# First head's values taken quad by quad beside its keys and queries, first operands in finer steps, decay steps at other ticks

## The chip, the cores and the metric

One core of one Trainium2 chip runs the kernel. The metric is the device time of one execution in microseconds; with several runs their median counts. TensorE (PE) multiplies matrices, VectorE (DVE) and ScalarE (ACT) work on elements, GpSimd (POOL) does some of that too, and SyncE (SP) issues most transfers.

## The reference

One decoder block over 256 tokens of width 2048, all in float32. RMS norm, then one wide projection `w_in` gives queries, keys and values of four heads, a low-rank decay, and gates; gated linear attention runs in chunks of 64 tokens; its normed output is merged with a gated short convolution; an output projection, a second norm and a SwiGLU network follow. What matters here is the attention's front:

```python
proj = jnp.einsum('bsd,de->bse', h, w_in)
(q, k, v, g_out, gk_low, ...) = jnp.split(proj, SPLIT_IDX, axis=-1)
gk = jnp.einsum('bsr,rk->bsk', gk_low, w_gk_up) + b_gk_up
log_g = jax.nn.log_sigmoid(gk.astype(jnp.float32)) / GATE_LOGIT_NORMALIZER
...
bcum = jnp.cumsum(gc, axis=3)
q_dec = qc * jnp.exp(bcum)
k_dec = kc * jnp.exp(-bcum)
scores = jnp.einsum('nbhik,nbhjk->nbhij', q_dec, k_dec)
scores = jnp.where(causal, scores, 0.0)
o_intra = jnp.einsum('nbhij,nbhjv->nbhiv', scores, vc)
```

The decay `log_g` of all heads is needed before the scores of the first head.

## The kernel before

**Split operands.** Each float32 operand is held as a high part and a low part that PE takes. ACT writes the high part (`hi` from `raw`, L238), DVE the low part (`lo`, L243: raw minus hi). `mm3` (L345 to L349) issues three matmuls per product: low by high, high by low, high by high.

**The weight stream.** Weights come in pieces of 512 KB (128 partitions by 1024 numbers) in the order of `stream_list`. `load_piece` (L268) takes a `raw` buffer of five, issues the load on SP and records ACT's `hi`; DVE's `lo` is recorded one piece later (`finish_low`), from six `hi` and five `lo` buffers. `take` keeps five pieces ahead of use. For keys and queries a piece holds four steps of 128 rows by 256 columns, for values two by 512 columns. The first piece alone is loaded and split in two halves.

**x.** The transposed, gain-scaled x stands as `xh` and `xl` (16 steps of 128 by 256). `start` (L512) loads some steps into a `raw` buffer and splits them, ACT for `xh` and DVE for `xl`. `hooks` say ahead of which piece (and which half of it) a `start` is recorded; `split_gkw` does the same for the decay's low-rank weights. `load_x` reads x once more by token (`xq`) for its square sums, which give the row factor `r1` and, spread by a small product on PE, `rb`.

**Ticks.** Every used piece is one tick. `later` and `at` hang a function on a tick. The order of each engine's instructions is then a list, and an engine takes its list in that order.

**The first head.** `mm_cols(["k0", "q0"], ...)` (L474) takes k0 and q0 piece by piece in turn, eight ticks, with the low-rank decay product `gk_chunks` (L579, eight matmuls each time) behind each k piece. The head's values v0 follow through `mm_tok`, eight ticks. At tick 13 `split_low` and `scale_rows` run, at 14 and 15 `decay_logits` (PE writes `zp`, ACT `za`, DVE `zm`), at 17 the Sigmoid, at 19 `log_decay` (Ln, and DVE's sum), at 20 and 21 `sum_decay` (DVE scans), at 22 `tables_within` (DVE copies, Exp into `ek`), at 23 the Exp into `eq`, at 25 `tables_across` (POOL, then Exp into `exk` and `exq`). `decayed` (L751) multiplies them by the head's scaled keys and queries, from tick 27, and `scores` (L759) is at 29 for the first head, 30 for the second. Meanwhile k1, q1 and v1 go through PE.

**Banks.** Keys, queries and values take turns in six PSUM banks; `aux` gives two more in turn, to `gk_ps`, `rb_ps`, `zp`, `sc_ps` and `o_ps`.

The later heads, the gates, the output projection and the feed-forward network follow in the same stream and aren't touched.

## Time and profile before

| what | value |
|---|---|
| median of 3 runs | 1506.32 us (1505.82 to 1508.32) |
| the profiled execution's own time | 1505.39 us |
| its span in the profile | 1503.7 us |
| granted PE clock, mean | 0.998 |
| PE busy | 1488.9 us (99%) |
| DVE busy | 1277.6 us (85%) |
| ACT busy | 862.9 us (57%) |
| first product after the warm-up starts at | 5.45 us |
| first head's scores start at | 94.87 us |

The span runs from the first to the last instruction; the own time has 1.7 us around it. A row of the timeline gives start, duration, engine, line, operation, output and inputs by name, count, and in brackets the idle time before it with what ended it. PE's rows overlap, since a matmul's end is modelled while the next one already runs: what one matmul costs is read from start to start. A row of the waits gives who waited for whom, the total, the number and the longest.

### The profile page before, as it was taken

What the parts mean: (1) busy time and instruction counts of PE and PEld (TensorE: products, weight loads), DVE (VectorE), ACT (ScalarE), POOL (GpSimd) and SP (SyncE); (2) the same over time, 40 slices, a digit from 0 to 9 for tenths busy, and PEclk for the clock granted to TensorE, in tenths of its full rate; (3) what the DMA queues carried; (4) which work ended last, traced back from release to release, by engine and by line L of the source; (5) the groups of instructions that cost most, each with busy time, mean ns of one, the idle gap of its engine ahead of it and who ended that gap; (6) DMA issues with size and microseconds to landing.
All of it is one profiled execution on the core that took longest, in us unless ns stands there. A gap on an engine that the chain in (4) does not pass through costs nothing.

```text
span 1503.7 us, 19350 instructions
## 1 busy us (share of the span) xinstructions
PE 1488.9 (99%) x7057; PEld 1244.0 (83%) x7057; DVE 1277.6 (85%) x1280; ACT 862.9 (57%) x975; POOL 33.1 (2%) x60
## 2 busy tenths in 40 slices
PE   9999999999999999999999999999999999999997
PEld 8989988888887888888888888888888788888886
DVE  5885869979979879966689999999999999999975
ACT  6864546655655655654566756655565556565553
POOL 0010000000000000000000000000000000000000
PEclk9999999999999999999999999999999999999999
DMA  9755557877877877786676777777877777786782
GB/s 312 239 171 171 178 162 257 283 229 234 283 261 232 296 247 248 252 261 214 211 222 214 238 249 252 252 263 226 268 238 238 256 265 273 243 268 224 241 288 84
DMA packets 99984, 358.58 MB, mean 238 GB/s; under 512 B 11476, under 2 KB 11604, under 8 KB 99760
## 3 DMA queue, kind: packets, MB, share of 16 engines
q1 hardware_dynamic: 96656, 346.88, 70.0%
q0 software_dynamic: 2800, 8.89, 2.2%
q10 hardware_dynamic: 432, 1.57, 0.3%
q8 instruction: 55, 0.90, 0.2%
q14 instruction: 41, 0.34, 0.1%
HBM read 351.03 MB, written 2.10 MB: 235 GB/s over the span
## 4 chain that ended last, share of the span: by engine, by line
PE 95%; DVE 2%; issue 1%; ACT 1%; DMA 0%; SPq 0%; DVEq 0%; ACTq 0%
PE fg L347 8%; PE fg L349 8%; PE fg L348 8%; PE dn L347 5%; PE dn L349 5%; PE dn L348 5%; PE gc L347 3%; PE gc L348 3%; PE gc L349 3%; PE wo L347 2%; PE wo L349 2%; PE v L347 2%; PE gb L347 2%; PE wo L348 2%; PE v L348 2%; PE v L349 2%
## 5 line engine op out<-in xcount | busy, mean ns | idle before, releaser
L243 DVE TENSOR_TENSOR lo<-raw,hi 128x1024 fp32r<-128x1024 f32 (+1 forms) x505 | 611.6, 1219 | 114.3 <-ACT hi L238 32.3
L238 ACT CAST hi<-raw 128x1024 fp32r<-128x1024 f32 (+1 forms) x505 | 523.9, 1048 | 272.5 <-PE gb L349 25.9
L238 ACT CAST hi<-x 128x1024 fp32r<-128x1024 f32 x144 | 151.7, 1053 | 263.5 <-DVE x L265 201.0
L243 DVE TENSOR_TENSOR lo<-x,hi 128x1024 fp32r<-128x1024 f32 x144 | 176.1, 1223 | 37.8 <-ACT hi L238 26.3
L347 PE MATMUL dn<-lo,acth 128*128 128x512 f32 (+1 forms) x368 | 140.7, 382 | 1.7 <-DVE h L1043 0.9
L349 PE MATMUL dn<-hi,acth 128*128 128x512 f32 (+1 forms) x368 | 139.9, 380 | 0.0
L348 PE MATMUL dn<-hi,actl 128*128 128x512 f32 (+1 forms) x368 | 139.8, 380 | 0.0
L265 DVE TENSOR_TENSOR x<-x,raw 128x1024 f32<-128x1024 f32 x96 | 117.0, 1219 | 11.3 <-DMA raw<-in_w_in_dram 6.2
L347 PE MATMUL fg<-lo,hh 128*128 128x512 f32 x288 | 112.4, 390 | 0.0
L349 PE MATMUL fg<-hi,hh 128*128 128x512 f32 x288 | 112.2, 390 | 0.0
L348 PE MATMUL fg<-hi,hl 128*128 128x512 f32 x288 | 112.1, 389 | 0.0
L347 PE MATMUL fg<-lo,sh 128*128 128x512 f32 x256 | 101.0, 395 | 0.0
L348 PE MATMUL fg<-hi,sl 128*128 128x512 f32 x256 | 99.9, 390 | 0.0
L349 PE MATMUL fg<-hi,sh 128*128 128x512 f32 x256 | 99.8, 390 | 0.0
L347 PEld LDWEIGHTS dn<-lo,acth 128*128 128x128 f32 x368 | 69.2, 188 | 15.7 <-DVE h L1043 1.7
L349 PEld LDWEIGHTS dn<-hi,acth 128*128 128x128 f32 x368 | 69.2, 188 | 13.3
L348 PEld LDWEIGHTS dn<-hi,actl 128*128 128x128 f32 x368 | 69.2, 188 | 12.9
L347 PEld LDWEIGHTS fg<-lo,hh 128*128 128x128 f32 x288 | 54.1, 188 | 11.7 <-DVE lo L243 0.5
L349 PEld LDWEIGHTS fg<-hi,hh 128*128 128x128 f32 x288 | 54.1, 188 | 11.3
L348 PEld LDWEIGHTS fg<-hi,hl 128*128 128x128 f32 x288 | 54.1, 188 | 11.1
L259 DVE TENSOR_TENSOR raw<-y,x 128x1024 f32<-128x1024 f32 x48 | 58.5, 1219 | 4.4 <-DMA y<-in_w_gu_dram 2.5
L243 DVE TENSOR_TENSOR lo<-y,hi 128x1024 fp32r<-128x1024 f32 x48 | 58.5, 1218 | 4.3 <-ACT hi L238 2.2
(246 smaller groups left out, 3063.4 us busy)
## 6 DMA issues: line engine op xcount, KB each, us to landing
raw<-in_w_in_dram SPq DMA_DIRECT2D x255, 512.0 KB, 4.6
raw<-in_w_gu_dram SPq DMA_DIRECT2D x176, 512.0 KB, 4.4
raw<-in_w_dn_dram SPq DMA_DIRECT2D x88, 512.0 KB, 4.5
x<-in_w_gu_dram SPq DMA_DIRECT2D x32, 512.0 KB, 4.9
y<-in_w_gu_dram SPq DMA_DIRECT2D x32, 512.0 KB, 3.8
raw<-in_w_out_dram SPq DMA_DIRECT2D x32, 512.0 KB, 3.8
y<-in_w_in_dram SPq DMA_DIRECT2D x16, 512.0 KB, 4.6
x<-in_w_in_dram SPq DMA_DIRECT2D x16, 512.0 KB, 4.8
```

Of the source, the lines that this page charges most:

```text
L238: nc.scalar.copy(hi[:, ks, :], raw[:, ks, :])
L243: nc.vector.tensor_tensor(out=lo[:, ks, :], in0=raw[:, ks, :], in1=hi[:, ks, :].bitcast(F32), op=ALU.subtract)
L259: nc.vector.tensor_tensor(out=raw, in0=y, in1=held["x"], op=ALU.add)
L265: nc.vector.tensor_tensor(out=x, in0=x, in1=other, op=ALU.add)
L347: nc.tensor.matmul(ps, lhsT=sh, rhs=ml, start=first, stop=False, skip_group_check=onto)
L348: nc.tensor.matmul(ps, lhsT=sl, rhs=mh, start=False, stop=False, skip_group_check=onto)
L349: nc.tensor.matmul(ps, lhsT=sh, rhs=mh, start=False, stop=last, skip_group_check=onto)
```

## The change

Four edits, all in the head of the program. What is computed stays the same, and PE has the same matmuls.

- The stream takes k0, q0 and two pieces of v0 in turn (a quad of four steps of the contraction), four times. `mm_cols` gets `beside`: it takes the two value pieces after the queries' and puts the low-rank decay product behind the second of them. v0's two banks are thus in use from the start, beside k0's and q0's four. `done` scales keys and queries two ticks after their last piece.
- The first piece is loaded and split in steps of one, one and two, the second in two halves, and x's first four steps in one, one and two. The gain columns are loaded on ACT's queue instead of SP's. `split_gkw` is recorded ahead of piece 3, and x's next quarters ahead of pieces 4, 7 and 11.
- The decay steps: `split_low` 13 to 17, logits 14 and 15 to 18 and 19, Sigmoid 17 to 20, `log_decay` 19 to 21, `sum_decay` 20 and 21 both to 22, tables 22 to 23, Exp 23 to 24; `tables_across` stays at 25. `decayed` and `scores` keep their ticks.
- v0's high and low parts are written at tick 20 instead of straight after its last piece.

```diff
-    first = [p for pair in zip(out[0], out[1]) for p in pair]
-    return first + [p for g in out[2:] for p in g]
+    first = [p for k, q, v, w in zip(out[0], out[1], out[2][0::2], out[2][1::2]) for p in (k, q, v, w)]
+    return first + [p for g in out[3:] for p in g]
...
-                step = n // 2 if i == 0 else n
+                cuts = {0: (0, 1, 2, n), 1: (0, 2, n)}.get(i, (0, n))
...
-                for a in range(0, n, step):
-                    b = a + step
+                for a, b in zip(cuts, cuts[1:]):
...
-    def mm_cols(keys, ah, al, each=None):
+    def mm_cols(keys, ah, al, beside=None, each=None, done=None):
 
         ps = {key: [bank([P, T], f"{key}_{m}") for m in range(2)] for key in keys}
+        if beside:
+            ps[beside] = [bank([P, 512], f"{beside}_{t}") for t in range(NT)]
         for k0 in range(0, KC, 4):
             for key in keys:
                 col_piece(ps[key], take(key, k0), k0, ah, al)
-                if each and key == keys[0]:
+                if done and k0 == KC - 4:
+                    later(2, lambda key=key: done(key, ps[key]))
+                used()
+            for k in (k0, k0 + 2) if beside else ():
+                piece = take(beside, k)
+                for t in range(NT):
+                    tok_piece(ps[beside][t], t, piece, k, k == 0, k == KC - 2, whole(ah, al))
+                if k > k0:
                     each(k0)
                 used()
...
+        if a == 0:
+            nc.scalar.dma_start(cols, cols_in)
         nc.sync.dma_start(xs[:, 0:b - a, :], xt[:, a * T:b * T].rearrange("p (k t) -> p k t", t=T))
-        if a == 0:
-            nc.sync.dma_start(cols, cols_in)
...
-    hooks[(0, 0)] = lambda: start(xs0, 0, 2)
+    hooks[(0, 0)] = lambda: start(xs0, 0, 1)
+    hooks[(0, 1)] = lambda: start(xs0[:, 1:2, :], 1, 2)
     hooks[(0, 2)] = lambda: start(xs0[:, 2:4, :], 2, 4)
-    hooks[(1, 0)] = split_gkw
+    hooks[(3, 0)] = split_gkw
...
-    at(13, split_low)
+    at(17, split_low)
     for i in range(4):
-        at(14 + i // 2, lambda i=i: decay_logits(2 * i))
-    at(17, lambda: nc.scalar.activation(za, za, AF.Sigmoid))
-    at(19, log_decay)
-    at(20, lambda: sum_decay(0))
-    at(21, lambda: sum_decay(4))
-    at(22, tables_within)
-    at(23, lambda: first_exp.append(nc.scalar.activation(eq, eq, AF.Exp, scale=inv).ins))
+        at(18 + i // 2, lambda i=i: decay_logits(2 * i))
+    at(20, lambda: nc.scalar.activation(za, za, AF.Sigmoid))
+    at(21, log_decay)
+    at(22, lambda: sum_decay(0))
+    at(22, lambda: sum_decay(4))
+    at(23, tables_within)
+    at(24, lambda: first_exp.append(nc.scalar.activation(eq, eq, AF.Exp, scale=inv).ins))
     at(25, tables_across)
...
+        if i:
+            values()
+        else:
+
+            at(20, values)
```

The order on the engines. PE first, at the last of the decay's logits `zp`. Before, they stand among the last matmuls of v0 (`v_0`, `v_1` are its two banks):

```order
L347 MATMUL v_0_516<-lo,xh 128x512
L348 MATMUL v_0_516<-hi,xl 128x512
L349 MATMUL v_0_516<-hi,xh 128x512
L670 MATMUL zp<-gks,gus 128x256 x2
L347 MATMUL v_1_517<-lo,xh 128x512
L670 MATMUL zp<-gks,gus 128x256 x2
L348 MATMUL v_1_517<-hi,xl 128x512
```

In the changed program they stand between the third and the fourth piece of k1 (`k_0`, `k_1` are its banks):

```order
L345 MATMUL k_1_696<-xl,hi 128x256
L346 MATMUL k_1_696<-xh,lo 128x256
L347 MATMUL k_1_696<-xh,hi 128x256
L691 MATMUL zp<-gks,gus 128x256 x4
L345 MATMUL k_0_695<-xl,hi 128x256
L346 MATMUL k_0_695<-xh,lo 128x256
L347 MATMUL k_0_695<-xh,hi 128x256
```

All eight logits' matmuls moved from v0 into k1, in two groups of four (the first group stands one piece of k1 earlier). `scores`, at the end of the decay chain, kept its place: behind 60 matmuls of v1.

ACT next, from the Ln's table load to the last Exp, before:

```order
L691 ACT_TABLE_LOAD
L691 ACTIVATE za_501<-za_501 128x2048
L238 CAST hi_822<-raw_821 128x1024
L238 CAST hi_858<-raw_857 128x1024
L238 CAST hi_892<-raw_891 128x1024
L238 CAST hi_927<-raw_926 128x1024
L706 ACT_TABLE_LOAD
L706 ACTIVATE ek_505<-eq_504 128x2048
L238 CAST hi_958<-raw_957 128x1024
L734 ACTIVATE eq_504<-eq_504 128x2048
L238 CAST hi_996<-raw_995 128x1024
L720 ACTIVATE exk_1013<-exk_1013 128x1024
```

And in the changed program:

```order
L712 ACTIVATE za_682<-za_682 128x2048
L238 CAST hi_891<-raw_890 128x1024
L238 CAST hi_929<-raw_928 128x1024
L238 CAST hi_964<-raw_963 128x1024
L238 CAST hi_1003<-raw_1002 128x1024
L238 CAST hi_1030<-raw_1029 128x1024
L727 ACT_TABLE_LOAD
L727 ACTIVATE ek_686<-eq_685 128x2048
L238 CAST hi_1048<-raw_1047 128x1024
L755 ACTIVATE eq_685<-eq_685 128x2048
L741 ACTIVATE exk_1020<-exk_1020 128x1024
L742 ACTIVATE exq_1021<-exq_1021 128x1024
```

The cast between the Exp into `eq` and that into `exk` is gone; the casts between Ln and the first Exp became five. Ahead of the Ln's table load, where two casts stood behind the Sigmoid, one stands now.

DVE last, from the table copies to the first head's products with `eq` and `exq`, before:

```order
L705 COPY eq_504<-bc_503 128x8x64
L243 TENSOR_TENSOR lo_930<-raw_891,hi_892 128x1024
L243 TENSOR_TENSOR lo_961<-raw_926,hi_927 128x1024
L806 TENSOR_TENSOR kr_987<-k1_0_726,rb_114 128x256
L806 TENSOR_TENSOR kr_987<-k1_1_727,rb_114 128x256
L755 TENSOR_TENSOR ek_505<-ek_505,kr_514 128x512
L807 SCALAR_TENSOR_TENSOR qr_988<-q1_0_855,rb_114 128x256
L807 SCALAR_TENSOR_TENSOR qr_988<-q1_1_856,rb_114 128x256
L243 TENSOR_TENSOR lo_999<-raw_957,hi_958 128x1024
L755 TENSOR_TENSOR eq_504<-eq_504,qr_515 128x512
L243 TENSOR_TENSOR lo_1026<-raw_995,hi_996 128x1024
L755 TENSOR_TENSOR exk_1013<-exk_1013,kr_514 128x256
```

And in the changed program:

```order
L726 COPY eq_685<-bc_684 128x8x64
L673 SCALAR_TENSOR_TENSOR qr_997<-q1_0_856,rb_114 128x256
L673 SCALAR_TENSOR_TENSOR qr_997<-q1_1_857,rb_114 128x256
L243 TENSOR_TENSOR lo_1006<-raw_963,hi_964 128x1024
L243 TENSOR_TENSOR lo_1033<-raw_1002,hi_1003 128x1024
L243 TENSOR_TENSOR lo_1051<-raw_1029,hi_1030 128x1024
L776 TENSOR_TENSOR ek_686<-ek_686,kr_632 128x512
L776 TENSOR_TENSOR eq_685<-eq_685,qr_653 128x512
L243 TENSOR_TENSOR lo_1073<-raw_1047,hi_1048 128x1024
L776 TENSOR_TENSOR exk_1020<-exk_1020,kr_632 128x256
L776 TENSOR_TENSOR exq_1021<-exq_1021,qr_653 128x256
L776 TENSOR_TENSOR eq_685<-eq_685,qr_997 128x512
```

The scaling of k1 (`kr_987` before) went ahead of the table copies. Three low parts of weights stand between the last table copy and the product with `eq` in both, now in one run; one stands between the product with `eq` and that with `exk`, as before. Of v1's pieces, `lo_1006` is the fifth's low part.

## The prediction
> **What bounds the kernel now.** I read the page first, then the waits of TensorE (PE), then PE by stage, then the timeline of the start and of the decay steps.

> The page's busy row and the first row of its chain:

> ```profile
> PE 1488.9 (99%) x7057; PEld 1244.0 (83%) x7057; DVE 1277.6 (85%) x1280; ACT 862.9 (57%) x975; POOL 33.1 (2%) x60
> ...
> PE 95%; DVE 2%; issue 1%; ACT 1%; DMA 0%; SPq 0%; DVEq 0%; ACTq 0%
> ```

> PE is busy 99% of 1503.7 us and is 95% of the chain that ended last. The change leaves PE the same matmuls, so only PE's waiting can change. A busy PE isn't a PE at full pace, though, so stretches by the granted clock and count come next:

> ```profile
> 5.45:11.89 6.44, 5.48 (x35) 4.65 (x35) 3.86 (x7) 3.86 (x8) 0.00 (x0) 1.00 0.96 350
> 11.89:58.38 46.49, 46.49 (x300) 42.46 (x301) 33.74 (x52) 35.32 (x58) 0.31 (x1) 1.00 0.93 319
> 58.38:81.41 23.03, 23.03 (x193) 23.03 (x193) 19.17 (x22) 14.54 (x14) 4.29 (x3) 1.00 0.51 147
> 81.41:95.03 13.62, 13.62 (x62) 11.26 (x62) 13.05 (x19) 11.95 (x11) 2.50 (x3) 1.00 0.47 155
> ```

> The columns are PE, weight loads, DVE, ACT, POOL, then clock, DMA share and GB/s. Only the first stretch has idle PE. From 11.89 to 95.03 PE never stops; DVE works 13.05 of the last 13.62 us. So in the start there is something to win, and up to the scores at 95 there is nothing to win and much to lose. The waits of PE say the same: the one in the start is small, and the longest anywhere after the warm-up is 0.9 us.

> ```profile
> PE g L347 <- DVE lo L243: 0.9, 1, 0.9
> ...
> PE k L347 <- DVE xl L519: 0.6, 1, 0.6
> ```

> **The start.** The timeline of the first 13 us, PE and what it waits for:

> ```profile
> 1.26 0.42 SPq L515 DMA_DIRECT2D cols<-in_cols_dram  x1
> 1.27 4.02 PE L500 MATMUL warm_ps<-warm 128*128 128x512 bf16 x9 [1.27 <-DVE spare L496]
> 3.94 0.91 ACT L518 ACTIVATE xh<-xs,cols 128x256 fp32r<-128x256 f32 x2 [1.64 <-DMA cols<-in_cols_dram]
> 5.45 0.80 PE L347 MATMUL k<-xl,hi 128*128 128x256 f32 x2 [0.16 <-ACT hi L238]
> 8.38 0.50 PE L347 MATMUL k<-xl,hi 128*128 128x256 f32 x2 [0.60 <-DVE xl L519]
> 9.10 0.38 PE L348 MATMUL k<-xh,lo 128*128 128x256 f32 x1 [0.23 <-DVE lo L243]
> 11.89 0.38 PE L348 MATMUL q<-xh,lo 128*128 128x256 f32 x1
> 12.23 0.28 PE L348 MATMUL q<-xh,lo 128*128 128x256 f32 x1
> 12.35 0.28 PE L349 MATMUL q<-xh,hi 128*128 128x256 f32 x1
> ```

> From 12.23 to 12.35 a 256-column matmul takes 0.12 us. By 11.89 PE has started 24 of k0, 8 of the decay's low-rank product (gk) and 2 of q0: 34, worth 4.1 us, in 6.44 us. Some 2.3 us are lost, and the warm-up (to 1.27 + 4.02 = 5.29) forbids a start much before 5.45. So **2.4 us is the most the start can give**.

> The new steps let the first quarter of k0 begin as the warm-up ends instead of 0.16 later, but the wait at 8.38 to 9.10 is for the second half of x and of the piece, and ahead of it stand as many bytes as before (two steps of 128 KB in place of each 256 KB). What smaller steps cost in transfer, the trace shows only by its neighbours:

> ```profile
> 3.00:4.00 1.00, 1.00 (x4) 0.40 (x3) 0.00 (x0) 0.06 (x1) 0.46 (x3) 1.00 0.85 265
> ...
> 6.00:7.00 1.00, 1.00 (x7) 0.83 (x6) 0.12 (x1) 0.10 (x1) 0.00 (x0) 1.00 0.87 200
> ```

> At 3 to 4 us rows of 2 KB move at 265 GB/s; at 6 to 7, with the 128 KB of gkw among them, 200. For the 512 KB now cut to 1-KB rows this is 2.6 instead of 1.9 us at worst; nothing at best. I take 0.3, nearer the middle since gkw was only part of the mix. Then the lower half of k0 starts at 9.10 + 0.3 = 9.4, its last ten matmuls take 1.2 to 10.6, and q0 follows at once, because gk now stands behind the values and q0 comes in halves. By 11.89 PE has done 24 + 1.29/0.12 = 35 against 34: **0.1 us won**. The bounds are 0.7 lost (the worst transfer rate, plus a little) and 2.4 won.

> Edits of the start that I cost at nothing: the columns' load on ACT's queue saves SP one 0.42 us issue and delays ACT by about as much, under ACT's 1.64 idle; without that cover, 0.4. The gkw split goes three pieces later and is needed only after the first values. From there each quad gives PE 48 matmuls at 0.12, 24 at 0.23 (13.62 us for the 60 of v1 up to 95.03) and 8 at 0.12, 12.2 us for 2.5 MB, where it had 6.7 us for 1.5 MB: less demand per us than the 350 GB/s above, so no transfer is late.

> **The decay chain.** Here is the larger term. PE's anchors first:

> ```profile
> 51.59 0.64 PE L670 MATMUL zp<-gks,gus 96*128 96x256 f32 x4
> ...
> 56.82 0.40 PE L670 MATMUL zp<-gks,gus 96*128 96x256 f32 x2
> ...
> 58.22 0.28 PE L347 MATMUL k<-xl,hi 128*128 128x256 f32 x1
> ...
> 81.24 0.40 PE L347 MATMUL v<-lo,xh 128*128 128x512 f32 x1
> ...
> 94.87 1.05 PE L766 MATMUL sc_ps<-eq,ek 128*128 128x128 f32 x8
> 95.76 0.61 PE L768 MATMUL sc_ps<-exq,exk 128*128 128x128 f32 x4
> ```

> Now zp, the decay's logits, stands in the middle of v0; the last pair starts at 56.82 and the first head's scores at 94.87: **38.0 us** for everything between. In the new order the last zp stand after three of k1's four pieces. Moving 8 of them behind v0 lets k1 start 1.0 earlier, at 57.2, less the 0.1: 57.1. Two pieces of k1 (48 x 0.12 = 5.8), four zp (0.5), one piece (2.9): the second group begins at 66.3, its last pair at 66.5. That pair waits for the readers of the first group, which use the same two banks. The reader's row in the next fence, 53.94, ends 3.2 after the group's start at 51.59, and one DVE pass over a logit ends some 0.4 later; PE is back after 28 x 0.12 = 3.4. I take 0.1, between 0 and 0.5: last pair at 66.6, **9.7 later** than before. The scores, with the same PE work ahead of them, would come at 94.87 - 0.1 + 0.1 = 94.9. So only 28.3 us remain.

> What the chain needs is in the rows of ACT, DVE and POOL, each of which takes its instructions in the order of its list:

> ```profile
> 53.94 0.87 ACT L673 ACTIVATE za<-zp,cols 128x256 f32<-128x256 f32 x2 [0.32 <-DVE zm L674]
> ...
> 60.57 1.28 ACT L729 ACT_TABLE_LOAD   x1
> ...
> 63.69 1.98 ACT L238 CAST hi<-raw 128x1024 fp32r<-128x1024 f32 x2
> 65.68 1.28 ACT L691 ACT_TABLE_LOAD   x1
> ...
> 83.07 1.28 ACT L706 ACT_TABLE_LOAD   x1 [6.34 <-DVE eq L705]
> ...
> 87.13 1.92 ACT L734 ACTIVATE eq<-eq 128x2048 f32<-128x2048 f32 x1
> 88.94 1.03 ACT L238 CAST hi<-raw 128x1024 fp32r<-128x1024 f32 x1
> 89.88 1.06 ACT L720 ACTIVATE exk<-exk 128x1024 f32<-128x1024 f32 x1
> ```

> ```profile
> 68.92 2.29 DVE L692 TENSOR_TENSOR zm<-zm,za 128x2048 f32<-128x2048 f32 x1 [0.72 <-ACT za L691]
> ...
> 82.16 0.83 DVE L705 COPY eq<-bc 128x512 f32<-128x512 f32 x1
> ...
> 87.98 1.21 DVE L243 TENSOR_TENSOR lo<-raw,hi 128x1024 fp32r<-128x1024 f32 x1
> 89.11 0.68 DVE L755 TENSOR_TENSOR eq<-eq,qr 128x512 f32<-128x512 f32 x1
> ...
> 91.92 0.43 DVE L755 TENSOR_TENSOR exq<-exq,qr 128x256 f32<-128x256 f32 x1 [0.34 <-ACT exq L721]
> ```

> ```profile
> 82.68 1.23 POOL L718 TENSOR_TENSOR exq<-bc 128x512 f32<-128x512 f32 x1
> ```

> From the last zp pair (56.82) to the end of eq x qr (89.11 + 0.68 = 89.79) the chain took 33.0, and to the end of exq x qr (91.92 + 0.43) 35.5. It fitted with 5 us to spare. It isn't loose: each link starts as the one before ends (68.92 on Ln, 83.07 on the copy at 82.16 + 0.83). Fewer ticks between steps therefore don't shorten it; only fewer strangers in the queues do. The new lists take out two: one of the two casts at 63.69 (0.95) and the cast at 88.94 (0.94). The other weight splits stay, one between zm and the scans, one behind the scans.

> So: the Ln sum 68.92 + 9.7 - 0.95 = 77.7; the Exp table load 83.07 + 8.75 = 91.8; **eq x qr 97.9 to 98.5**, where PE is at 94.9. Behind it DVE now has one weight split (1.13, by 87.98 to 89.11), exk (0.4) and exq (0.43): **exq ready at 100.5**. PE's second set of score matmuls would start at 95.76 + 0.0 = 95.8. **4.7 us lost.** Before that the same queue is late once more: the fifth piece of v1 needs a split that stands behind the table copies (91.8 - 0.1) and two scalings of q1, done near 93.6, where PE is at 92.1. So PE would wait 1.5, 2.2 and 1.0 us in three places, one sum of 4.7.

> Bounds of this term: 3.9 if the handovers between engines shrink by 0.8 in all, 5.5 if DVE falls behind by most of one more split (1.13). Nothing takes it back later: PE has no slack behind the scores. POOL's five table operations end at 83.9 now, at 92.7 then, 5 us before exk's Exp at 97.7: hidden. v0's accumulators hold six banks with k0's and q0's; k1 needs k0's, scaled about 7 us ahead of it; v1 needs v0's, read around 70 against 81: hidden, each with over 5 us.

> [...] The 0.9 us wait above left the clock at 1.00. [...]

> **Sum.** 1505.39 (the profiled execution; its span is 1503.7, 1.7 lies around it) - 0.1 + 0.1 + 4.7 = 1510.1. The median shown, 1506.32, is 0.9 above that execution, so I forecast **1511.0** for a median.

> **Rivals.**
> - The chain fits after all (not slower). For: the steps stand closer in ticks, and DVE's 19.17 of 23.03 and ACT's 14.54 leave gaps. Against: the links are chained by data, and the gaps lie in waits for the chain itself. It decides at the slack: last zp pair to exq must shrink from 35.5 to 29.2, and two casts give only 1.9. Then only the start counts: 1506.2, or 1503.9 if the start wins all. Chance 0.14.
> - The change's start wins its full 2.4 with the chain as I say: 1511.0 - 2.3 = 1508.7. It is inside the range and in the forecast's chance.
> - The three waits run together and the clock falls. The start shows the cold pace: 0.80 for two matmuls at 5.45, 0.50 at 8.38. A cold stretch like the start's (1.27 to about 6.2) at half pace costs 2.5: 1513.5. Chance 0.06, as three waits are likelier than one.

> That the instructions stand otherwise than described is no rival: the lists are the program's own.

> **How the numbers follow.** Forecast 0.80. The range runs from 1511.0 - 2.7 (chain 3.9, two of the start's 2.4) to 1511.0 + 2.6 (chain 5.5, start 0.7 lost, or the clock): 1508.3 to 1513.6; it leaves out the first rival and tails. A measurement of this kernel can tell about 0.2%, 3.0 us. Faster than that would need more than the start holds: 0.02. Within: 0.12 of the first rival and 0.03 of the forecast's lower edge, 0.15. Slower: 0.83.

> **What would show it.** After the change: zp in k1; the Exp table load near 92; DVE's eq x qr ending near 98.5; PE waits of about 1.5 on a weight split in v1 and of 2.2 and 1.0 on DVE eq and exq at the scores; k1 starting near 57. I am wrong if PE reaches the scores without a wait, if k1 starts more than 1 us off 57.1, or if the granted clock falls below 1.00 there.

## The result and the profile after

| | before | after |
|---|---|---|
| median of 5 runs each | 1506.32 us (1505.23 to 1508.32) | 1514.21 us (1511.18 to 1515.28) |
| ratio of the times, 95% interval | | 1.0049 (1.0037 to 1.006) |
| the profiled execution's own time | 1505.39 us | 1514.47 us |
| its span | 1503.7 us | 1512.8 us |

The change makes the kernel slower, by 7.9 us of the medians (0.5%; the interval of the ratio lies wholly above 1) and 9.1 us of the two profiled executions. The page of after, its busy row and the first row of its chain:

```profile
PE 1490.8 (99%) x7057; PEld 1243.8 (82%) x7057; DVE 1278.4 (85%) x1282; ACT 863.0 (57%) x977; POOL 33.0 (2%) x60
...
PE 85%; DVE 6%; issue 3%; DMA 2%; ACT 2%; SPq 0%; DVEq 0%; ACTq 0%
```

The busy row tells nearly nothing, as before. In the chain PE's share fell from 95% to 85%, but this row scatters too: the later profiles of the unchanged kernels have 93% and 90% for before and 93%, 93% and 89% for after. The waits of PE in after name the places. Three are new between 90 and 101 us: 1.4 of the first row (its other 0.88 us lies in the start), and the other two rows:

```profile
PE v L345 <- DVE lo L243: 2.2, 2, 1.4
...
PE sc_ps L787 <- DVE eq L776: 1.7, 1, 1.7
...
PE sc_ps L789 <- DVE exq L776: 0.6, 1, 0.6
```

The timeline of after at the points that the prediction named, PE, ACT and DVE:

```profile
57.45 0.28 PE L345 MATMUL k<-xl,hi 128*128 128x256 f32 x1
...
66.57 0.80 PE L691 MATMUL zp<-gks,gus 96*128 96x256 f32 x4
...
92.06 1.28 ACT L727 ACT_TABLE_LOAD   x1 [6.45 <-DVE eq L726]
...
98.05 0.69 DVE L776 TENSOR_TENSOR eq<-eq,qr 128x512 f32<-128x512 f32 x1 [1.20 <-ACT eq L755]
...
92.29 0.39 PE L347 MATMUL v<-hi,xh 128*128 128x512 f32 x1
94.04 0.50 PE L345 MATMUL v<-lo,xh 128*128 128x512 f32 x1 [1.36 <-DVE lo L243]
...
96.67 0.39 PE L347 MATMUL v<-hi,xh 128*128 128x512 f32 x1
98.80 1.16 PE L787 MATMUL sc_ps<-eq,ek 128*128 128x128 f32 x8 [1.74 <-DVE eq L776]
100.61 0.60 PE L789 MATMUL sc_ps<-exq,exk 128*128 128x128 f32 x3 [0.65 <-DVE exq L776]
```

What a wait costs is read from start to start: 92.29 to 94.04 is 1.75, less the 0.23 that a matmul of 512 columns takes, 1.52 us. The bracket says 1.36, since it counts from the modelled end at 92.29 + 0.39. In the same way the three waits are 1.5, 1.9 and 0.8, together **4.2 us**. The first product behind each wait takes another 0.1 us more than usual (94.04 to 94.38, against 0.23).

The same markers in both timelines show where the rest came:

| start of | before | after | later by |
|---|---|---|---|
| k1 (before: less the 1.0 of the zp that stood ahead) | 57.22 | 57.45 | 0.23 |
| v1 | 81.24 | 81.61 | 0.37 |
| the first scores | 94.87 | 98.80 | 3.93 |
| the first head's `o_ps` | 103.02 | 107.97 | 4.95 |
| the first `g` | 204.25 | 209.20 | 4.95 |
| the same `dn` group near the end | 1447.59 | 1456.17 | 8.58 |
| end of the span | 1503.7 | 1512.8 | 9.1 |

Here `o_ps` is the first product of scores and values, `g` a product of the gates and `dn` one of the feed-forward network's last projection. Up to the first `o_ps` the program lost what the start (0.4 up to v1) and the waits explain. Then nothing for 100 us; then 3.6 us between `g` and `dn`, where the lists of all engines are the same in both kernels. The first theory was that the chain is late for its place on PE (C), which explains the 4.95. For the other 4 us there were two rivals: it belongs to the change (P), or it is scatter of single transfers (S). A third one, the clock (H), came only with the second profile of the changed kernel.

### The profile page after: what moved, and what is told of

The parts are those of the page before. It is cut to its first block, busy times and chain, and to the rows that moved or that the text cites. A ratio compares the mean times of both kernels' runs of the same rounds, so it can differ in the third digit from the quotient of the medians.

```text
span 1512.8 us, 19359 instructions
## 1 busy us (share of the span) xinstructions
PE 1490.8 (99%) x7057; PEld 1243.8 (82%) x7057; DVE 1278.4 (85%) x1282; ACT 863.0 (57%) x977; POOL 33.0 (2%) x60
## 4 chain that ended last, share of the span: by engine, by line
PE 85%; DVE 6%; issue 3%; DMA 2%; ACT 2%; SPq 0%; DVEq 0%; ACTq 0%
PE fg L347 7%; PE fg L345 7%; PE fg L346 7%; PE dn L345 4%; PE dn L347 4%; PE dn L346 4%; DVE lo L243 3%; PE gc L345 3%; PE gc L346 3%; PE gc L347 3%; PE wo L345 2%; PE gb L345 2%; PE gb L347 2%; PE gb L346 2%; PE wo L346 2%
## 5 line engine op out<-in xcount | busy, mean ns | idle before, releaser
L243 DVE TENSOR_TENSOR lo<-raw,hi 128x1024 fp32r<-128x1024 f32 (+1 forms) x507 | 612.1, 1214 | 118.1 <-ACT hi L238 34.3
L238 ACT CAST hi<-raw 128x1024 fp32r<-128x1024 f32 (+1 forms) x507 | 524.2, 1045 | 280.1 <-PE gb L347 27.5
L238 ACT CAST hi<-x 128x1024 fp32r<-128x1024 f32 x144 | 151.6, 1053 | 270.9 <-DVE x L265 215.9
L243 DVE TENSOR_TENSOR lo<-x,hi 128x1024 fp32r<-128x1024 f32 x144 | 176.1, 1223 | 36.3 <-ACT hi L238 25.9
L347 PE MATMUL dn<-hi,acth 128*128 128x512 f32 (+1 forms) x368 | 139.9, 380 | 0.0
L347 PE MATMUL fg<-hi,hh 128*128 128x512 f32 x288 | 112.2, 390 | 0.0
L347 PE MATMUL fg<-hi,sh 128*128 128x512 f32 x256 | 99.8, 390 | 0.0
L347 PEld LDWEIGHTS dn<-hi,acth 128*128 128x128 f32 x368 | 69.2, 188 | 13.3
L347 PEld LDWEIGHTS fg<-hi,hh 128*128 128x128 f32 x288 | 54.1, 188 | 11.2
L243 DVE TENSOR_TENSOR lo<-y,hi 128x1024 fp32r<-128x1024 f32 x48 | 58.5, 1219 | 4.6 <-ACT hi L238 2.1
```

Of the source, the lines that this page charges most:

```text
L238: nc.scalar.copy(hi[:, ks, :], raw[:, ks, :])
L243: nc.vector.tensor_tensor(out=lo[:, ks, :], in0=raw[:, ks, :], in1=hi[:, ks, :].bitcast(F32), op=ALU.subtract)
L347: nc.tensor.matmul(ps, lhsT=sh, rhs=mh, start=False, stop=last, skip_group_check=onto)
```

## The experiments

Sixteen runs in five comparisons, each with its own runs of the kernel before on the same chip. "Above before" means the difference of the medians within one comparison.

### Does the later loss belong to the change?

The two kernels, run again without any edit.

> The kernel before, unchanged, a second profile and more times. In the first profile of it PE goes from the start of the first o_ps matmul (103.02) to the start of the last dn group (1447.59) in 1344.6 us; in the changed kernel, whose lists of instructions are the same there, in 1348.2. Theory S (scatter: single transfers that land up to 1 us late at places that differ from run to run): this profile lies anywhere from 1343 to 1349 for the same stretch, with waits of PE over 0.3 us at other places than the first time, and the time 1505 to 1508.5. Theory P (the 3.6 us belong to the change): the stretch takes 1344.6 within 0.6 again, with its waits at the same places.

Measured: 1506.88 us on both sides (ratio 0.9998, 0.999 to 1.0007). The stretch from `o_ps` to `dn` took 1346.4 us, 1.8 longer than in the first profile. The places of the waits were mostly the old ones, against what S said, but their sizes weren't: the one ahead of the last `trb` group but one (transposes on PE) went from 0.5 to 1.5 us.

The second repeat was made later, beside runs on the first steps; theory G, that finer first steps cost about 1 us somewhere behind, is taken up there.

> The kernel before, unchanged, for comparison. All theories: within 0.5 of the other runs of it; theory G: 1243.3 to 1244.7 us from the first g matmul to the last dn group.

Measured: 1507.14, beside 1507.3 for the other runs. One row of the stage view, from the first `g` to the `dn` group, for three kernels: before, this second repeat of before, and after. The columns are length, PE, weight loads, DVE, ACT, POOL, clock, DMA share, GB/s.

```profile
204.25:1447.59 1243.34, 1239.84 (x5527) 1021.43 (x5525) 1098.62 (x1036) 715.12 (x770) 22.20 (x39) 1.00 0.75 248
```

```profile
204.00:1451.10 1247.10, 1241.29 (x5527) 1021.86 (x5525) 1097.74 (x1035) 714.30 (x769) 22.13 (x39) 1.00 0.76 247
```

```profile
209.20:1456.17 1246.97, 1241.36 (x5526) 1021.07 (x5525) 1098.78 (x1035) 713.82 (x768) 22.15 (x39) 1.00 0.76 247
```

The unchanged kernel before can take 1247.1 us for the stretch too: **S holds**, the 3.6 us are within the kernel's own scatter. From the first `o_ps` to `dn` the three profiles of before take 1344.6, 1346.4 and 1348.3 us, and the four of the changed kernel 1348.2, 1347.6, 1345.1 and 1347.4. One piece of the scatter, in before and in after, as DVE waits for a transfer or doesn't (SPq is the issue, DVE the first reader):

```profile
1052.32 0.33 SPq L232 DMA_DIRECT2D y<-in_w_gu_dram  x1
...
1057.04 1.23 DVE L259 TENSOR_TENSOR raw<-y,x 128x1024 f32<-128x1024 f32 x1
```

```profile
1058.42 0.33 SPq L232 DMA_DIRECT2D y<-in_w_gu_dram  x1
...
1064.10 1.23 DVE L259 TENSOR_TENSOR raw<-y,x 128x1024 f32<-128x1024 f32 x1 [0.93 <-DMA y<-in_w_gu_dram]
```

The issue comes 6.1 later in after, as all of PE does there, but DVE's step comes 7.1 later: the transfer landed some 1 us late. DVE is busy 88% of the whole stretch (1098.8 of 1247.0), so it has little room to make that up. Some 60 us on, at 1126.82, PE waits 0.6 for DVE in after and not in before; that this is the same delay come through is argued, not shown.

> The changed kernel, unchanged, a second profile and more times. All theories: the three waits before and at the scores come again at 1.5, 1.9 and 0.8 us within 0.2, and the first o_ps matmul starts 4.9 to 5.0 us later than in the kernel before. Theory S: the stretch from the first o_ps to the last dn group takes anywhere from 1343 to 1349 us, and the median of all its times comes nearer to 4.9 above that of the kernel before (1511.5 to 1512.5). Theory P: the stretch takes 1348.2 within 0.6 again, waits at the same places, and the median stays at 1514.

Measured: 1514.8 us, 7.9 above before, from 1510.5 to 1518.3, and 1347.6 us for the stretch. Taken alone this run is as P wanted it, in the stretch and in the median; it is the repeats of before and the later ones of this kernel that rule P out. The profile had something that no theory expected. Its timeline of PE at the scores:

```profile
57.41 0.28 PE L345 MATMUL k<-xl,hi 128*128 128x256 f32 x1
...
97.45 1.16 PE L787 MATMUL sc_ps<-eq,ek 128*128 128x128 f32 x8 [2.10 <-DVE eq L776]
99.26 1.22 PE L789 MATMUL sc_ps<-exq,exk 128*128 128x128 f32 x4 [0.65 <-DVE exq L776]
...
109.53 0.39 PE L345 MATMUL o_ps<-vl,sch 128*128 128x512 f32 x1
```

and its stages, cut where the clock changes:

```profile
95.21:98.63 3.42, 1.31 (x9) 0.97 (x8) 3.42 (x4) 2.48 (x3) 1.64 (x2) 1.00 0.77 256
98.63:102.04 3.41, 2.78 (x9) 2.39 (x10) 3.41 (x7) 2.14 (x3) 0.00 (x0) 0.50 0.46 165
102.04:105.45 3.41, 3.41 (x10) 2.64 (x9) 2.78 (x5) 0.78 (x2) 0.31 (x1) 0.50 0.67 168
```

The clock is the third number from the end. The wait on the fifth v1 piece is gone and the other two are 2.3 and 0.8 from start to start (3.1 us in all, less than in the first profile), yet `o_ps` comes at 109.53, 1.6 later. The clock column says why: it is 0.50 from 98.63 to 105.45. That is theory H, which all later runs test: **behind the waits the clock falls, in some runs.**

> The changed kernel, unchanged, beside the next two on one chip. Theory H (waits of 3.1 to 4.2 us, and in most runs, not in all, a fallen clock behind them at about 3 us): a median 6.5 to 8.5 above the kernel before, times that spread over more than 3 us, and lower clocks where the time is longer. Theory N (no clock, late transfers): the spread is that of the kernel before.

Measured: 1512.38, 5.0 above before (1509.8 to 1515.7): below the 6.5 to 8.5 of H, but with the wide spread that H wanted (5.9 us, beside 2.4 in the kernel before). In this profile the same rows read:

```profile
57.10 0.28 PE L345 MATMUL k<-xl,hi 128*128 128x256 f32 x1
...
97.15 1.16 PE L787 MATMUL sc_ps<-eq,ek 128*128 128x128 f32 x8 [2.10 <-DVE eq L776]
...
106.33 0.39 PE L345 MATMUL o_ps<-vl,sch 128*128 128x512 f32 x1
```

```profile
92.96:96.37 3.41, 2.09 (x10) 1.39 (x8) 3.41 (x3) 2.67 (x2) 3.41 (x3) 1.00 0.66 217
96.37:99.79 3.42, 2.00 (x14) 1.76 (x15) 3.42 (x6) 3.21 (x4) 0.17 (x1) 1.00 0.69 181
```

Two executions of one kernel, with the same waits (2.1 on eq, 0.65 on exq by the brackets). With the clock at 1.00, k1 to `o_ps` takes 106.33 - 57.10 = 49.2 us; with the fallen clock 109.53 - 57.41 = 52.1. The difference, **2.9 us, is the clock alone**.

> The changed kernel, unchanged, beside the run before. Theory S and H: one of the two patterns of VectorE and GpSimd, waits of 3.1 or 4.2 us with it, and in about two runs of three a clock of 0.997 or less; runs at 0.996 or less 2.5 to 3.5 us above those at 0.998.

Measured: 1511.62, 5.4 above before (ratio 1.0035, 1.0021 to 1.0049). The waits are those of the two repeats before; the clock fell again, this time for 3.4 us, and k1 to `o_ps` takes 50.9, 1.6 more than with a full clock:

```profile
95.81:99.22 3.41, 1.66 (x13) 1.48 (x13) 3.41 (x6) 2.88 (x4) 0.50 (x1) 1.00 0.82 184
99.22:102.64 3.42, 3.42 (x10) 2.75 (x10) 3.42 (x7) 1.56 (x4) 0.00 (x0) 0.50 0.36 137
```

Over all 22 runs of the changed kernel, 15 have a mean clock of 0.997 or less, against 6 of 119 of the kernel before. The 7 at 0.998 are on average 5.1 us above before, the 9 at 0.997 5.9, the 6 at 0.996 or less 8.6: the 3.5 between the first and the last group is at the upper end of what the expectation gave, the middle group is only 0.8 above the first. The mean clock is a coarse gauge here: in the profiles the program's end, behind the last product, lies at half clock for 4.2 to 7.0 us, which alone moves the third digit.

### Take the waits away, or lengthen them

The first edit puts scores and the products with the values one tick later, the second two ticks:

```diff
-        at(max(now + 3, 29 + i), lambda i=i: scores(i))
+        at(max(now + 3, 30 + i), lambda i=i: scores(i))
...
-        tick_of = max(count["tick"] + 1, 31)
+        tick_of = max(count["tick"] + 1, 32)
```

> The changed kernel with the scores and the products with the values one tick (one weight piece, 2.9 us of PE) later, and nothing else. Theory C (the decay chain is late for its fixed place on PE, 4.2 of the 4.9 us): the waits on eq and exq (1.9 and 0.8) go, the wait on the fifth v1 piece (1.5) stays, since its split stands where it stood; the head's end comes 2.7 us earlier than in the changed kernel, and the time is 2.5 to 3 us below it, 2 above the kernel before. Rival D (what PE lacks is DVE's work, so a wait taken away at the scores comes back at the next thing that DVE owes PE): waits of about 2.7 us show again at scr, scl, or a weight split within the next 15 us, and the time is the changed kernel's.

Measured: 1509.39, 2.5 above before (ratio 1.0016, 1.0007 to 1.0025) and 5.4 below the changed kernel in the same comparison, about twice what C expected. The wait on eq is gone, waits of 0.5 on exq and 0.9 on `scr` (the scores as they are copied out of PSUM) were left, and the wait on the fifth v1 piece, which C kept, isn't there, as in the three repeats of the changed kernel. The clock was 0.998 or more in all 11 runs. D in its full form falls: what is left is 1.3 us and the time isn't the changed kernel's. That the gain is more than the waits taken away fits H.

> The changed kernel with the scores and the products with the values two ticks later. One tick later left waits of 0.46 at exq and 0.87 at scr ahead of the values' products, the clock at 0.998, and 1509.4. Theory C+H: no wait over 0.3 us from 90 to 125, and the time is 1506.5 to 1508.2, the kernel before within what a measurement can tell. Rival D (the 2.5 us that were left are not waits at the scores): 1509 to 1510 again.

Measured: 1507.82, 1.5 above before (1.0009, 1.0001 to 1.0018), one wait of 0.7 left, where C+H wanted none over 0.3, and the clock at 0.998 in all 11 runs. The time is as C+H said.

The third edit goes the other way, for the first head's scores alone:

```diff
-        at(max(now + 3, 29 + i), lambda i=i: scores(i))
+        at(max(now + 3, 29 + i) - (i == 0), lambda i=i: scores(i))
```

> The changed kernel with the first head's scores one tick earlier: the products with eq stand 12 matmuls (2.7 us of PE) earlier, those with exq 8. The wait on eq grows to 4.6 to 5.0 us in one piece, that on exq shrinks to under 0.3: 1.9 us more of waiting in all. Theory H: one gap of that length drops the clock in every run, for as long as in the second profile of the changed kernel (6 us at half pace, 3 us lost), so the median is 1.9 us plus the share of runs that keep the clock now, 2.5 to 3.5 above the changed kernel's. Theory N: 1.9 above it, at a clock of 1.00 behind the gap.

Measured: 1516.3, 8.9 above before and 3.9 above the changed kernel in the same comparison, a little over H's range. All 5 runs had a clock of 0.995 or 0.996. The wait and the stages of this profile:

```profile
98.72 2.08 PE L787 MATMUL sc_ps<-eq,ek 128*128 128x128 f32 x8 [6.11 <-DVE eq L776]
```

```profile
93.57:96.98 3.41, 0.00 (x0) 0.00 (x0) 3.22 (x4) 3.41 (x3) 0.00 (x0) 1.00 0.56 150
96.98:100.39 3.41, 1.67 (x8) 1.67 (x9) 2.41 (x4) 3.41 (x4) 0.00 (x0) 0.50 0.82 302
100.39:103.81 3.42, 3.42 (x12) 2.94 (x12) 1.70 (x5) 1.33 (x2) 0.00 (x0) 0.50 0.55 168
```

One gap of 6.1 us: the clock falls 4.4 us into it, at 96.98, and stays down until 103.81, 5.1 us after PE has work again. The wait was 6.1 and not 5.0 since this profile has the long pattern of the decay steps (below).

### Keep the waits, but not the idleness

Throwaway products fill the two waits; PE waits as long for eq and exq as before.

```diff
+        for n in range(16 if i == 0 else 0):
+            nc.tensor.matmul(ps[:, 0:2, :], lhsT=xh[:, n, 0:P], rhs=xh[:, n, :], start=True, stop=True)
         for t in range(NT):
...
+        for n in range(5 if i == 0 else 0):
+            nc.tensor.matmul(ps[:, 2, :], lhsT=xh[:, n, 0:P], rhs=xh[:, n, 0:P], start=True, stop=True)
         for j, m in enumerate(ms):
```

> The changed kernel with throwaway matmuls ahead of the first head's scores, into the scores' own accumulators, which the real ones then overwrite: 16 of 256 columns ahead of eq (about 1.9 us at full pace) and 5 of 128 columns ahead of exq (0.5 us). PE waits as long for eq and exq as before, but isn't idle meanwhile. Theory H (a part of the loss is the clock: in the second profile of the changed kernel, after waits of 2.1 and 0.65 us, the granted clock is 0.50 to 0.66 from 98 to 106, which costs about 3 us): the clock stays at 1.00 there in the profile and the time falls by 2 to 3 us below the changed kernel's, to 1511.5 to 1512.8. Theory N (the clock falls for another reason, or the rest is late transfers): the time stays at 1514 to 1515.

Measured: 1511.48, 5.1 above before. The stages of the scores in its profile:

```profile
93.23:96.65 3.42, 3.42 (x23) 3.11 (x22) 3.42 (x3) 2.51 (x2) 3.42 (x3) 1.00 0.82 200
96.65:100.06 3.41, 3.07 (x23) 2.67 (x22) 3.41 (x6) 3.37 (x4) 0.01 (x1) 1.00 0.58 156
```

PE is never idle for long and the clock stays at 1.00. From k1 to the first `o_ps` the profile takes 49.2 us, as long as the second repeat of the changed kernel, which had the same waits and kept its clock: what the throwaway products can save is the clock and nothing else. The time is where H put it, but the changed kernel wasn't run on that chip, so it was run again beside it.

> The changed kernel with throwaway matmuls in the waits ahead of the first head's scores, again, now with the changed kernel beside it on the same chip. Theory H: the clock is 0.998 or 0.999 in nearly all its runs and its median 1.5 to 3 below the changed kernel's. Theory N: its median is that of the changed kernel within 0.8.

Measured: 1511.82, 4.4 above before, only 0.6 below the changed kernel of that comparison: that is N's outcome, and not the 1.5 to 3 of H. The changed kernel had 0.998 in 4 of its 6 runs there, so there was less to win; by the medians of this comparison alone H isn't shown. What stands is the clock: 13 of the 15 runs with filled waits have 0.998 or more, against 7 of 22 without.

### What decides whether the clock falls

The stages quoted here are cut at the changes of the clock, and they have one length: behind the waits the clock was low for 3.41 or 6.83 us, never for another time. Counted in steps of 3.413 us from the moment at which the clock first rose in that execution (5.67 in after, 6.47 in its first repeat, 4.21 in the second), every fall and rise lies on a step (from the first rise to the fall at the end of the program after takes 1501.86 us, 440 steps, and before 1491.62, 437). So cut, the two cells of after that hold its waits read:

```profile
94.42:97.83 3.41, 2.64 (x12) 1.84 (x10) 2.43 (x3) 3.41 (x3) 0.00 (x0) 1.00 0.70 209
97.83:101.25 3.42, 1.80 (x13) 1.61 (x14) 3.20 (x6) 3.42 (x5) 0.00 (x0) 1.00 0.82 268
```

The cell with the least work of PE near the scores (from 80 to 130 us) in each profile, and the clock in the cell behind it:

| profile | PE busy in its emptiest cell of 3.41 us | clock in the next |
|---|---|---|
| scores one tick earlier | 0.00 | 0.50 |
| GpSimd held back (below) | 1.19 | 0.50 |
| after, first repeat | 1.31 | 0.50 |
| decay's ticks alone (below) | 1.32 | 0.50 |
| after, third repeat | 1.66 | 0.50 |
| after | 1.80 | 1.00 |
| coarse start (below) | 1.90 | 1.00 |
| after, second repeat | 2.00 | 1.00 |
| filled waits, second time | 2.19 | 1.00 |
| scores one tick later | 2.70 | 1.00 |
| filled waits, first time | 3.07 | 1.00 |

So it is in all eleven profiles with waits at this place: where PE was busy for 1.66 us or less in a cell at full clock, the next had 0.50, and where it was busy for 1.80 or more, 1.00. Behind the waits the clock rose again after a cell that was nearly full: not after 1.67 (scores one tick earlier) or 2.78 (after, first repeat), but after 3.05 (GpSimd held back), 3.23 (decay's ticks alone), 3.41 and 3.42. At the start of the programs it rose after 3.26 in before and 3.41 in after, elsewhere once after 2.94 (after, second repeat) and once after 2.99, but not after 3.08 and 3.21 in two others, so busy time alone doesn't tell the rise. Since the cells began at another moment in each execution, the same waits fell into one cell (1.31 in the first repeat of after) or were shared by two (2.09 and 2.00 in the second). The limit for the fall, between 1.66 and 1.80, was read from these rows, and no run was made to test it, but the rest of the traces does. All 18 profiles together have 7886 such cells at full clock. The 23 with half clock behind them (5 at these waits, 18 at the ends of the programs) hold 0.00 to 1.66 us of work, and every other one holds 1.80 or more (in before 437 cells, the last with 0.04 and the others with 2.48 or more; in after 440, the last with 0.00 and the others with 1.80 or more).

### One part of the change alone

The decay's ticks alone, in the kernel before, with the old order of pieces and the old start:

```diff
-    at(13, split_low)
+    at(17, split_low)
     for i in range(4):
-        at(14 + i // 2, lambda i=i: decay_logits(2 * i))
-    at(17, lambda: nc.scalar.activation(za, za, AF.Sigmoid))
-    at(19, log_decay)
-    at(20, lambda: sum_decay(0))
-    at(21, lambda: sum_decay(4))
-    at(22, tables_within)
+        at(18 + i // 2, lambda i=i: decay_logits(2 * i))
+    at(20, lambda: nc.scalar.activation(za, za, AF.Sigmoid))
+    at(21, log_decay)
+    at(22, lambda: sum_decay(0))
+    at(22, lambda: sum_decay(4))
+    at(23, tables_within)
...
```

> The kernel before with only the decay's steps moved to the ticks of the changed kernel; the values behind keys and queries and the first steps as before. Theory C+H (the whole loss is the late chain, as waits of 3 to 4.3 us in all and as a fallen clock behind them): about the changed kernel's time, 1512.5 to 1515, with waits on eq and exq at the scores. Rival Q (the values side by side, or the finer steps, cost a share of their own): 1509 to 1511.5, waits or not.

Measured: 1511.55, 5.2 above before (1.0031, 1.0019 to 1.0042): below C+H's range in absolute terms, at Q's upper edge, but as far above before as the changed kernel was in its last two comparisons. All 6 runs had a clock of 0.997. From k1 to the first `o_ps` its profile takes 51.1 us, 5.3 more than before (there less the 1.0 of `zp`): the whole loss. PE waits 0.3 on eq and 0.5 on exq by the brackets, and longest on a weight split of v1, where C+H had the waits at the scores. The longest wait and the stages behind it:

```profile
94.25 0.50 PE L347 MATMUL v<-lo,xh 128*128 128x512 f32 x1 [2.09 <-DVE lo L243]
```

```profile
92.07:95.48 3.41, 1.32 (x6) 1.05 (x6) 3.41 (x5) 3.19 (x3) 1.04 (x1) 1.00 0.20 23
95.48:98.90 3.42, 3.23 (x8) 1.97 (x6) 3.36 (x4) 3.42 (x4) 0.00 (x0) 0.50 0.72 280
```

A single wait of 2.1 us was enough here, and the clock fell 1.2 us after PE had work again.

The other four runs are about the first steps. First the changed kernel with the first steps of before (cuts in halves for k0 only, q0 whole, two chunks of x, the columns on SP):

```diff
-                cuts = {0: (0, 1, 2, n), 1: (0, 2, n)}.get(i, (0, n))
+                cuts = (0, n // 2, n) if i == 0 else (0, n)
...
-    hooks[(0, 0)] = lambda: start(xs0, 0, 1)
-    hooks[(0, 1)] = lambda: start(xs0[:, 1:2, :], 1, 2)
+    hooks[(0, 0)] = lambda: start(xs0, 0, 2)
```

> The changed kernel with the first steps of before: k0's first piece in two halves, q0's whole, x two chunks at a time, the columns on SP's queue; the quads and the decay's new ticks stay. Theory C+H: the start is worth under 1 us either way, the waits at the scores and the fallen clock are as in the changed kernel, and the time is 1513.5 to 1515.5. Rival Q (the finer steps cost a share): 1511.5 to 1513.

Measured: 1512.05, 5.7 above before (1.0032, 1.0021 to 1.0044), the two waits at 2.1 and 0.65, the clock below 0.998 in 3 of 6 runs. k1 starts at 58.15, 0.7 to 1.3 later than in the four profiles of the changed kernel (56.85 to 57.45): with the values side by side, the finer steps do win that much (in the last run below, coarse too, k1 starts at 58.01). They win it against the coarse quads, though, not against the old order, where k1 starts at 56.8 to 57.2, less the `zp`. The time lies in Q's range and not in that of C+H, but it is about as far above before as the changed kernel in two of its comparisons (5.0 and 5.4), and the changed kernel wasn't run on this chip: no share of the finer steps can be read from it.

Then the finer steps alone in the kernel before (`cuts`, the two `start` hooks and the columns on ACT's queue as in the change, nothing else), in two comparisons:

> The kernel before with the finer first steps alone: k0's first piece in three parts and q0's in two, x in steps of one chunk at first, the columns on ACT's queue; the order of the pieces, the values behind keys and queries, and the decay steps as before. Theory C: no wait at the scores; the second group of k0 matmuls starts 0.3 to 0.8 us earlier than 14.62, and the time is 1505.5 to 1506.3, no difference that a measurement of the time can tell. Rival F (the finer steps themselves cost transfer rate): the second group of k0 starts later than 14.62, by up to 0.7, and the time is up to 1507.

> The kernel before with the finer first steps alone, once more: its 1.0 above the kernel before (from 0.5 below to 2.1 above) was not told from no change. Theory G (the finer steps cost about 1 us, not at the start but in later waits): 0.7 to 1.5 above the kernel before again, and 1244.7 to 1246 us from the first g matmul to the last dn group. Theory S (scatter): within 0.6 of the kernel before.

Measured: 1.0 above before (1.0006, 0.9997 to 1.0014) and 0.8 below (0.9998, 0.9989 to 1.0006). The second group of k0 starts at 14.70 and 14.42, against 14.62, 14.21 and 14.38 in the three profiles of before. The first of the two times is above the ranges of both C and F, the second 0.2 outside S on the fast side. So neither a win nor a cost can be told, and G falls: nothing was lost, and the stretch took 1244.3.

At last the scores two ticks later together with the coarse steps:

> The changed kernel with the scores two ticks later and with the first steps of before. With the finer steps it stood 1.5 above the kernel before. Theory G: the stretch from the first g matmul to the last dn group is 1243.3 to 1244.7, and the time 0.3 to 1.0 above the kernel before, as the coarse first steps start the quads some 0.9 later. Theory S: 1.5 to 2.4 above the kernel before.

Measured: 1507.51, 0.2 above before (1.0005, 0.9996 to 1.0014), the best of the variants of the changed kernel, but its stretch from `g` to `dn` took 1245.9 us, so not for G's reason. No variant beat the kernel before by more than its interval.

### Who holds up whom among DVE and GpSimd

The profiles of one kernel showed two patterns of the decay tables: the chain came 1 to 3 us sooner in one than in the other. This edit makes GpSimd wait for VectorE's last table step:

```diff
             nc.vector.tensor_copy(eq[:, :, (n + 1) * C:(n + 2) * C], ch(n + 1))
+        for name in ("exk", "exq"):
+            t = across[name[-1]] = gpool.tile([P, NM, P], F32, tag=name, name=name)
+            nc.gpsimd.tensor_copy(t[:, NM - 1, C - 1:C + 1], eq[:, NM - 1, T - 2:T])
```

> The changed kernel with GpSimd's five steps of the across tables held back until VectorE has written the four steps of eq (two copies of two elements, from eq into tiles that the tables then overwrite). The profiles so far have two patterns at this place: VectorE's four steps at 1.53, 1.26, 1.55, 0.83 us with GpSimd's first at 1.9, or at 0.68, 0.42, 0.69, 0.42 with GpSimd's first at 3.8. Theory S (the two engines hold each other up when they read there at once, and which of them is held up differs from run to run): with GpSimd behind, VectorE's steps take 0.68 and 0.42, the wait of 1.5 on the fifth v1 piece is gone, the wait on eq is 2.1 to 2.3, that on exq 0.6 to 1.5, as exq's table comes up to 1.5 later; PE waits 2.9 to 3.7 in all, and the median is that of the changed kernel or up to 1.5 below it. Rival O (VectorE is slow there for another reason): the slow pattern in this profile too, with 4.2 us of waits.

Measured: 1512.93, 6.8 above before (1.0044, 1.0031 to 1.0057). The first two table steps of DVE and the first of GpSimd, in after, in its first repeat, and in this kernel:

```profile
87.05 1.53 DVE L725 TENSOR_TENSOR eq<-bc 128x512 f32<-128x512 f32 x1
88.50 1.26 DVE L726 COPY eq<-bc 128x512 f32<-128x512 f32 x1
...
86.11 1.93 POOL L735 TENSOR_TENSOR exk<-bc 128x512 f32<-128x512 f32 x1 [26.72 <-DVE bc L717]
```

```profile
87.00 0.68 DVE L725 TENSOR_TENSOR eq<-bc 128x512 f32<-128x512 f32 x1
87.60 0.42 DVE L726 COPY eq<-bc 128x512 f32<-128x512 f32 x1
...
86.05 3.80 POOL L735 TENSOR_TENSOR exk<-bc 128x512 f32<-128x512 f32 x1 [26.71 <-DVE bc L717]
```

```profile
86.81 0.68 DVE L727 TENSOR_TENSOR eq<-bc 128x512 f32<-128x512 f32 x1
87.41 0.42 DVE L728 COPY eq<-bc 128x512 f32<-128x512 f32 x1
...
89.11 1.04 POOL L737 TENSOR_TENSOR exk<-bc 128x512 f32<-128x512 f32 x1
```

Apart from each other GpSimd's first step takes 1.04 and DVE's 0.68 and 0.42, as S expected; but DVE is at 0.68 in most unforced profiles too, so that half proves little. PE waited 2.8 us in one piece (2.6 by the bracket), on eq and not at all on exq, the clock fell in the profile and was 0.997 or less in all 5 runs, and the time was not below the changed kernel's (6.8 above before, against 5.4 in the same comparison). Which of the two engines is held up moves the waits between 3.1 and 4.2 us in the changed kernel and isn't the cause of the loss.

## Why the prediction was right in its waits and wrong in its size

- **The direction and the chain: right.** k1 was to start at 57.1 and did at 57.45; the last zp pair at 66.6, measured in the group at 66.57; the Exp table load at 91.8, measured 92.06; eq x qr to end by 97.9 to 98.5, measured 98.74; exq at 100.5, and PE's products with it start at 100.61. The waits were to be 1.5, 2.2 and 1.0, 4.7 in all, and were 1.5, 1.9 and 0.8, 4.2. There is luck in this: the profile of before and the first of after share the pattern in which GpSimd slows DVE's table steps (1.5 instead of 0.7 us). In the three repeats it is the other way round, the first wait is gone, and the sum is 3.1, below the 3.9 that the prediction gave as its bound. That the late chain alone makes the loss is shown by the decay's ticks alone (5.2 above before), and that later scores give most of the time back is shown by the two shifts (2.5 and 1.5 above).
- **The start: within its bounds, its reasons half wrong.** 0.1 won was forecast, 0.2 lost was measured. The timeline of after's start, PE and ACT:

```profile
4.74 0.78 PE L345 MATMUL k<-xl,hi 128*128 128x256 f32 x1
...
7.56 0.51 PE L345 MATMUL k<-xl,hi 128*128 128x256 f32 x2 [0.61 <-ACT hi L238]
...
11.54 1.05 ACT L238 CAST hi<-raw 128x1024 fp32r<-128x1024 f32 x1 [0.86 <-DMA raw<-in_w_in_dram]
...
13.90 0.50 PE L345 MATMUL v<-lo,xh 128*128 128x512 f32 x1 [0.88 <-DVE lo L243]
```

  k0 starts at 4.74, earlier than "the warm-up forbids": the modelled end of the warm-up, 5.29, was no bound. "No transfer is late" was wrong for the first values: their piece landed late, and PE lost a microsecond at 13.90. The two errors nearly cancel. Over all profiles of the two unchanged kernels k1 starts at 56.8 to 57.2 before (less the `zp`) and at 56.9 to 57.5 after, so the start wins nothing.
- **The failed step: the third rival's condition.** "The three waits run together and the clock falls" had 0.06, "as three waits are likelier than one", and the sum gave the three waits no cost beside their length. That was the author's estimate: after the warm-up the trace of before had no wait over 0.9 us, and the clock stood at 1.00 there. Longer ones did cost more. Separate waits of 2.1 and 0.65 let the clock fall in two of four profiles of the changed kernel and lowered it in 15 of 22 runs, and a single wait of 2.1 did it in the decay's ticks alone: the waits need not run together; these left one cell with 1.31, 1.66 and 1.32 of 3.41 us of work, and behind it the clock was 0.50. The sum had the clock at nothing, and it cost some 1.5 us on average over the runs. The price of one fall, 2.5, was well guessed: 2.9 and 1.6 were measured.
- **"About 0.2%, 3.0 us" for what can be told, and the median.** The kernel before alone spreads from 1504.2 to 1511.7 over all comparisons, and its stretch from `g` to `dn` by 3.8 us. The first comparison, 7.9 above, was at the upper end: over four comparisons the changed kernel is 7.9, 7.9, 5.0 and 5.4 above before, and its 22 runs 5.5 by their median and 6.4 on average. The waits (3.1 to 4.2), the clock (about 2 in two thirds of the runs, some 1.5 on average) and the start make 5 to 6 of it. The profiled execution itself kept its clock: its 9.1 are 4.95 of waits and start, and 4.1 of the scatter behind them, which here fell high and in before's profile fell low (1247.0 and 1243.3 from `g` to `dn`, in a range of 1243.3 to 1247.1).

What stays open: the runs at a mean clock of 0.998 are on average 5.1 above before, 0.4 to 1.5 more than waits and start explain, and those at 0.997 only 0.8 more than these, where one low cell cost 1.6 in a profile. With single runs of one kernel spread over some 5 us, 22 runs don't settle it.

## What to carry to other kernels

Where a chain of steps ends at a fixed place of a full engine, moving its beginning by more than its slack costs about the difference, and it can be read before the change: 9.7 us later, 5 of slack, 3.1 to 4.2 of waits. Where waits leave PE with little work over a few us, even in pieces, add the clock as a cost with a real chance, not as a remote one: here it fell behind cells with 1.66 of 3.41 us of work and less, and cost 1.6 and 2.9 us. Before a difference is hunted through a long program, run the unchanged kernel twice: stretches with the same instructions differed by 3.8 us here.
